# A hybrid attention trunk: the FoX heads' reciprocal row sums go onto the outputs, by a PE transpose and a trip through DRAM, and no longer onto the probabilities

## The chip, the cores and the metric

One core of a Trainium2 chip runs the whole kernel. TensorE (PE) multiplies matrices and turns tiles, VectorE (DVE) and ScalarE (ACT) do elementwise work, and GpSimd (POOL) and SyncE (SP) mostly start transfers. Each engine has a queue of its own and works through it in order; semaphores make one wait for another. The metric is the device time of one execution in microseconds (us), lower is better.

## The reference

A trunk of two layers for one sequence of 512 tokens with 1024 channels, in fp32. Each layer adds half a SwiGLU feed-forward (width 2816), a mixer of two groups of heads, and a second half feed-forward to the residual x. The mixer has 4 differential heads and 8 FoX heads (forgetting attention) of 64 channels. What matters here is a FoX head:

```python
s_f = jnp.einsum('bhqd,bhkd->bhqk', qf, k_f).astype(jnp.float32) * scale_f
s_f = s_f + cf[..., :, None] - cum_f[..., None, :]
s_f = jnp.where(causal, s_f, -jnp.inf)
p_f = jax.nn.softmax(s_f, axis=-1)
o_f = jnp.einsum('bhqk,bhkd->bhqd', p_f.astype(v_f.dtype), v_f)
```

The softmax divides each query's row of exponentials by its sum. The division can stand on the probabilities, one number a query, before the product with v, or on the output after it.

## The kernel before

All fp32 products are made of three matmuls of rounded halves: an operand is split in a high half (a cast on ACT) and a low half (a subtraction on DVE), and hi·hi, hi·lo and lo·hi are summed in a PSUM bank (`mm3`, L386 to L391). Weights stream from DRAM through ring tiles and are split on arrival (L83 on ACT, L84 on DVE). The feed-forwards use a Strassen-like block scheme and take most of the time; PE is all but full there.

In the mixer (`mixer`) the attention of the twelve heads runs in steps, four query blocks of 128 a head, and between the steps PE is given other products, the "filler": the projections of heads still to come (reading XA, the normalised input's halves), FoX's v, and as far as they are ready the output projection's products (`out_early`). A table TARGET says how many filler matmuls should have been issued at each head. The heads come in order, 4 differential ones, then FoX heads 0 to 7. For each step s the loop calls:

- `trans_step(u, kb)` L869: PE turns the probability blocks of key block kb (128x128 each, L874) into one bank; ACT copies it as the high half (L883) and DVE subtracts for the low half (L884). The bank of kb=1 holds three blocks, 384 of its 512 columns.
- `softmax_step(u, qb)` L832: the scores of one query block (L824, L825 and the mask L827), then in the FoX branch DVE adds the forget gates and takes the row minimum (L860, an instruction and the read of its accumulator), ACT takes the exponential with the row sum as accumulator (L862), DVE takes the reciprocal of 128 sums (L863, 128x1) and ACT multiplies the block by it (L864).
- `pv_step(u, kb)`: the output products of key block kb (L913 and L914, v against the high and the low half). After the last, ACT moves a half (L943) and DVE adds it to the other (L944) in the tile `fo["u"]`, 64 partitions a head. The odd head of a pair then has `split_o` cut the pair's tile in halves y (L895 on ACT, L896 on DVE) for the output projection.

Last, `out_rest` multiplies the last pair of heads (6 and 7) and adds the mixer's result to x (L993).

The program order is not the engines' order: a scheduler in the tile layer orders each engine's queue by its own estimates, so a change of a few lines moves other instructions as well. The temporary tiles rotate: five banks for scores, turned blocks and outputs (`ps_b`), three for filler (`ps_a`), six of `t_tile`. SP's queue spreads each head's gates (L857) and loads weights. GpSimd's queue accumulates weight pairs of the feed-forwards (L134) and has nothing to do in FoX's part of the mixer.

Of the kernel before, what the change touches and what calls it, by code (L numbers as in the profile page):

```python
# [8 lines left out]
F32 = mybir.dt.float32  # L9
F32R = mybir.dt.float32r  # L10
BF16 = mybir.dt.bfloat16
AF = mybir.ActivationFunctionType
ALU = mybir.AluOpType
AX = mybir.AxisListType

P = 128
S = 512
# [5 lines left out]
FOX_H = 8  # L23
DIFF_H = 4
NB = S // P
# [22 lines left out]
def rf(t):  # L48
    return t.bitcast(F32)
# [3 lines left out]
def trunk(ctx, tc, xT, x, gains, gain_row, w_gu, w_dn, w_in, w_ff, w_out, fbias, lams, subln, consts, rope, out):  # L53
    nc = tc.nc
    act, dve, pool, pe, sp = nc.scalar, nc.vector, nc.gpsimd, nc.tensor, nc.sync
# [3 lines left out]
    sm = ctx.enter_context(tc.tile_pool(name="sm", bufs=4))  # L59
    ps = ctx.enter_context(tc.tile_pool(name="ps", bufs=1, space=bass.MemoryType.PSUM))  # L60
    dram = ctx.enter_context(tc.tile_pool(name="dram", bufs=2, space=bass.MemoryType.DRAM))
    turn = {}

    def nxt(key, n):
        i = turn.get(key, 0)
        turn[key] = i + 1
        return i % n
# [4 lines left out]
    def home(tag, shape, dt, name):  # L72
        return sb.tile(shape, dt, tag=tag, name=name, bufs=1)

    def t_tile(shape, dt, name, i=None):
        return home(f"t{nxt('t', 6) if i is None else i}", shape, dt, name)
# [139 lines left out]
    for n in range(2 * DEPTH):  # L216
        l = n // 2
        if n % 2 == 1:
            for i in range(24 + len(OUT_K)):
                k = OUT_K[i - 24] if i >= 24 else None  # L220
                tag = MIX[i % 3] if i < 24 else None if k >= 4 else MIX[(i - 28) % 3]
# [44 lines left out]
    ident = const.tile([P, P], F32, name="ident")  # L266
# [316 lines left out]
    def mixer(l, n_next, mid):  # L583
# [11 lines left out]
        pg = [home(f"G{3 + i}", [P, 2048], F32, f"pg{i}") for i in range(2)]  # L595
        PR = {3: 0, 2: 512, 1: 896, 0: 1152}

        def pr_tile(u, qb):
            w = (qb + 1) * P
            return pg[u % 2][:, PR[qb]:PR[qb] + w]  # L600

        def pm_tile():
            return pg[nxt("pm", 2)][:, 1280:1792]
# [212 lines left out]
        units = [("d", h) for h in range(DIFF_H)] + [("f", h) for h in range(FOX_H)]  # L816
        probs = [[] for _ in units]

        def scores(q1, kk, m, qb, masked):
            n = (qb + 1) * P  # L820
            w = max(n, 256)
            p = psum("b")
            lq = q1[m][:, qb * P:n]
            pe.matmul(p[:, 0:w], lq, kk[m][:, 0, 0:w], start=True, stop=False)  # L824
            pe.matmul(p[:, 0:w], lq, kk[m][:, 1, 0:w], start=False, stop=not masked)  # L825
            if masked:
                pe.matmul(p[:, qb * P:n], identb, maskb, start=False, stop=True)  # L827
            return p

        cbs = {}  # L830

        def softmax_step(u, qb):  # L832
            kind, h = units[u]
            n = (qb + 1) * P
            st = sm.tile([P, 6], F32, tag="st", name="st", bufs=6)
            if kind == "d":
                q1, kk = qk[("d", h)]
                pm = []
                for m in range(2):
                    p = scores(q1, kk, m, qb, False)  # L840
                    e = pr_tile(u, qb) if m == 0 else pm_tile()
                    dve.tensor_tensor_reduce(out=e[:, 0:n], in0=p[:, 0:n], in1=maskw[:, S - n:S], op0=ALU.add,
                                             op1=ALU.min, scale=1.0, scalar=3.0e38, accum_out=st[:, m:m + 1])
                    act.activation(out=e[:, 0:n], in_=e[:, 0:n], func=AF.Exp, scale=-1.0, bias=st[:, m:m + 1],
                                   accum_out=st[:, 2 + m:3 + m])
                    pm.append(e)
                dve.reciprocal(out=st[:, 4:6], in_=st[:, 2:4])
                dve.tensor_tensor(out=st[:, 5:6], in0=st[:, 5:6], in1=nlam, op=ALU.mult)
                act.mul(out=pm[1][:, 0:n], in_=pm[1][:, 0:n], mul=st[:, 5:6])
                dve.scalar_tensor_tensor(out=pm[0], in0=pm[0], scalar=st[:, 4:5], in1=pm[1][:, 0:n],  # L850
                                         op0=ALU.mult, op1=ALU.add)
                probs[u].append(pm[0])
            else:
                q1, kk = qk[("f", h // 2)]
                if qb == 0:
                    cbs[h] = rope_t[h % 2]
                    sp.dma_start(out=cbs[h], in_=cum_d[h:h + 1, :].partition_broadcast(P))  # L857
                p = scores(q1, kk, h % 2, qb, True)
                e = pr_tile(u, qb)
                dve.tensor_tensor_reduce(out=e, in0=p[:, 0:n], in1=cbs[h][:, 0:n], op0=ALU.add, op1=ALU.min,  # L860
                                         scale=1.0, scalar=3.0e38, accum_out=st[:, 0:1])
                act.activation(out=e, in_=e, func=AF.Exp, scale=-1.0, bias=st[:, 0:1], accum_out=st[:, 2:3])  # L862
                dve.reciprocal(out=st[:, 4:5], in_=st[:, 2:3])  # L863
                act.mul(out=e, in_=e, mul=st[:, 4:5])  # L864
                probs[u].append(e)

        pts = {}
# [1 line left out]
        def trans_step(u, kb):  # L869

            w = S - kb * P
            p = psum("b")
            for qb in range(kb, NB):
                pe.transpose(p[:, (qb - kb) * P:(qb - kb + 1) * P], probs[u][qb][:, kb * P:(kb + 1) * P], ident)  # L874
            if kb == NB - 1:
                th, tl = pt3
                dst = slice(P, 2 * P)
                full = (th, tl, slice(256, S))
            else:
                th, tl = pair()  # L880
                dst = slice(0, w)
                full = (th[:, 0:w], tl[:, 0:w], slice(kb * P, S))
            act.copy(out=th[:, dst], in_=p[:, 0:w])  # L883
            dve.tensor_tensor(out=tl[:, dst], in0=p[:, 0:w], in1=rf(th[:, dst]), op=ALU.subtract)  # L884
            pts[(u, kb)] = full
# [5 lines left out]
        fo = {}  # L891

        def split_o(i, u):
            oh, ol = y_pair(i)
            act.copy(out=oh, in_=u)  # L895
            dve.tensor_tensor(out=ol, in0=u, in1=rf(oh), op=ALU.subtract)  # L896
            ovt[i] = (oh, ol)

        def pv_step(u, kb):
            kind, h = units[u]  # L900
            if kb == 0:
                po_[u] = psum("b")
            po = po_[u]
            th, tl, cols = pts.pop((u, kb))
            hs = slice(h * P, (h + 1) * P)
            if kind == "d":
                vh, vl = vd[kb]
                pe.matmul(po[:, cols], vh[:, hs], th, start=kb == 0, stop=False)
                pe.matmul(po[:, cols], vl[:, hs], th, start=False, stop=False)
                pe.matmul(po[:, cols], vh[:, hs], tl, start=False, stop=kb == NB - 1)  # L910
            else:
                v = vf[kb][:, hs]
                pe.matmul(po[:, cols], v, th, start=kb == 0, stop=False)  # L913
                pe.matmul(po[:, cols], v, tl, start=False, stop=kb == NB - 1)  # L914
            if kb < NB - 1:
                return
            po_.pop(u)
            if kind == "d":
                o = os_[h // 2][:, h % 2]
                act.copy(out=o, in_=po)  # L920
                sq = t_tile([P, S], F32, "osq")
                act.activation(out=sq, in_=po, func=AF.Square)
                sh_, sl_ = pair()
                act.copy(out=sh_, in_=sq)
                dve.tensor_tensor(out=sl_, in0=sq, in1=rf(sh_), op=ALU.subtract)
                ov[h] = o

                def stats():
                    pq = psum("b")
                    pe.matmul(pq[0:32], ones[:, 0:32], sh_, start=True, stop=False)  # L930
                    pe.matmul(pq[0:32], ones[:, 0:32], sl_, start=False, stop=True)
                    act.activation(out=vv[32 * h:32 * h + 32], in_=pq[0:32], func=AF.Identity, scale=1.0 / P,
                                   bias=eps_t[0:32])
                    if h == DIFF_H - 1:
                        diff_norm()
                later.append(stats)
            else:
                if h % 2 == 0:
                    fo["u"] = pm_tile()
                own = slice(64 * (h % 2), 64 * (h % 2) + 64)  # L940
                oth = slice(64 - 64 * (h % 2), P - 64 * (h % 2))
                t = t_tile([P, S], F32, "fot")
                act.copy(out=t[own], in_=po[oth])  # L943
                dve.tensor_tensor(out=fo["u"][own], in0=po[own], in1=t[own], op=ALU.add)  # L944
                if h % 2 == 1:
                    split_o(h // 2, fo["u"])

        later = []
# [135 lines left out]
        for s in range(4 * len(units) + 5 + LAG):  # L1084
            u, i = divmod(s, 4)
# [6 lines left out]
            v, kb = divmod(s - 4 - LAG, 4)  # L1092
# [8 lines left out]
            v, kb = divmod(s - 5 - LAG, 4)  # L1101
# [327 lines left out]
```

## Time and profile before

| | |
|---|---|
| median of 3 runs | 1869.1 us (1868.81 to 1869.91) |
| profiled execution | 1871.02 us, its span 1869.2 us |
| granted TensorE clock, mean | 0.996 |
| scales on ACT (L864), both layers | 64, 35.9 us |
| reciprocals of 128x1 on DVE (L863) | 64, 10.2 us |
| transposes of probability blocks on PE (L874) | 240, 46.1 us |
| first output product of FoX head 0, layer 1 | 499 us from the span's start |
| last addition of head 7 (L944), layer 1 | 572.38 us |

A row of a group gives the line, the engine, the operation, out<-in tiles, the shapes and the count, then the busy time in us, the mean of one in ns, and the engine's idle time just before them with what ended it. A row of the timeline gives the start, the duration, the engine and the instruction; in brackets stands the idle time before it and what released it. A row of windows gives the length of a stretch and the busy time of each engine with its number of instructions, then the clock, the share of the DMA engines and GB/s. PE's matmuls are pipelined and their ends are modelled, so a busy PE may still wait; the distance between two starts is the better price.

### The profile page before, as it was taken

The page shows a single profiled execution, that of the slowest core. Times are in us where ns is not written, and L with a number is a line of the kernel's source. Part 1 is how long each engine was busy: PE and PEld are TensorE (multiplying, and loading weights), DVE is VectorE, ACT ScalarE, POOL GpSimd, SP SyncE. Part 2 cuts the span into 40 slices and gives each one's busy share as a digit, 9 for nine tenths or more (in the row PEclk, how much of TensorE's full clock was granted, in tenths as well). Part 3 has the DMA queues.
Part 4 walks back from the last instruction along what each step waited for, and adds up shares of the span by engine and source line. Part 5 has one row for each costly group of instructions (what it writes and reads, how often), then busy time and mean ns, then how long its engine had stood idle before and what let it go on. Part 6 is the DMA issues. An engine that isn't in the chain of part 4 may idle for free.

```text
span 1869.2 us, 24488 instructions
## 1 busy us (share of the span) xinstructions
PE 1833.9 (98%) x8702; PEld 1496.0 (80%) x8702; DVE 1611.6 (86%) x2528; ACT 1133.3 (61%) x1795; POOL 128.2 (7%) x154
## 2 busy tenths in 40 slices
PE   9999999999999999999999999999999999999997
PEld 5888888778868889888778988877777788888886
DVE  7898898778686999898998989997876869898998
ACT  7556555557795755565575556545576957455564
POOL 2010000000000100100001000000000000000101
PEclk9999999999999999999999999999999999999999
DMA  9787655243336775777567667533433466856742
GB/s 308 207 224 191 189 143 145 91 130 108 105 96 184 203 203 149 196 210 195 135 181 206 171 166 205 158 111 108 117 104 103 127 175 188 216 143 186 221 114 89
DMA packets 95529, 303.79 MB, mean 163 GB/s; under 512 B 12568, under 2 KB 15128, under 8 KB 95408
## 3 DMA queue, kind: packets, MB, share of 16 engines
q1 hardware_dynamic: 74816, 232.15, 37.1%
q0 software_dynamic: 19296, 68.17, 20.4%
q10 hardware_dynamic: 1296, 1.93, 0.4%
q8 instruction: 68, 1.11, 0.2%
q14 instruction: 53, 0.43, 0.1%
HBM read 287.45 MB, written 2.16 MB: 155 GB/s over the span
## 4 chain that ended last, share of the span: by engine, by line
PE 83%; DVE 9%; ACT 5%; DMA 2%; issue 1%; SPq 0%; DVEq 0%; ACTq 0%
PE ps_c L389 12%; PE ps_c L390 12%; PE ps_c L391 12%; PE ps L389 9%; PE ps L390 9%; PE ps L391 9%; PE ps_a L389 3%; PE ps_a L390 3%; PE ps_a L391 3%; DVE wg L84 2%; PE ps_t L485 2%; DVE x L514 1%; PE ps_g L1248 1%; PE ps_a L665 1%; PE ps_a L666 1%; PE ps_a L667 1%
## 5 line engine op out<-in xcount | busy, mean ns | idle before, releaser
L83 ACT CAST wg<-raw 128x1024 fp32r<-128x1024 f32 (+1 forms) x525 | 537.9, 1031 | 486.5 <-PE ps_c L391 188.9
L84 DVE TENSOR_TENSOR wg<-raw,wg 128x1024 fp32r<-128x1024 f32 (+1 forms) x525 | 619.7, 1190 | 105.5 <-ACT wg L83 104.0
L389 PE MATMUL ps_c<-wg,xf 128*128 128x512 f32 (+1 forms) x736 | 277.8, 378 | 2.2 <-ACT wg L83 1.3
L390 PE MATMUL ps_c<-wg,xf 128*128 128x512 f32 (+1 forms) x736 | 277.1, 377 | 1.0 <-DVE wg L84 1.0
L391 PE MATMUL ps_c<-wg,xf 128*128 128x512 f32 (+1 forms) x736 | 276.2, 376 | 0.0
L389 PE MATMUL ps<-wg,xf 128*128 128x512 f32 (+1 forms) x552 | 210.2, 381 | 0.0
L390 PE MATMUL ps<-wg,xf 128*128 128x512 f32 (+1 forms) x552 | 207.2, 376 | 0.0
L391 PE MATMUL ps<-wg,xf 128*128 128x512 f32 (+1 forms) x552 | 206.7, 376 | 0.0
L389 PEld LDWEIGHTS ps_c<-wg,xf 128*128 128x128 f32 x736 | 138.6, 188 | 29.2 <-ACT wg L83 1.7
L390 PEld LDWEIGHTS ps_c<-wg,xf 128*128 128x128 f32 x736 | 138.9, 189 | 26.5 <-DVE wg L84 1.5
L391 PEld LDWEIGHTS ps_c<-wg,xf 128*128 128x128 f32 x736 | 138.9, 189 | 25.1
L134 POOL DMA_DIRECT2D raw<-w_gu x86 | 74.6, 867 | 1137.8 <-DMA raw<-w_gu 640.3
L389 PE MATMUL ps_c<-wg,hf 128*128 128x512 f32 x352 | 138.5, 394 | 5.9 <-DVE x L514 5.8
L390 PE MATMUL ps_c<-wg,hf 128*128 128x512 f32 x352 | 137.4, 390 | 0.0
L391 PE MATMUL ps_c<-wg,hf 128*128 128x512 f32 x352 | 137.2, 390 | 0.0
L514 DVE SCALAR_TENSOR_TENSOR x<-ps_c,x 128x512 f32<-128x512 f32 x192 | 123.9, 680 | 1.3 <-PE ps_c L391 1.2
L391 PEld LDWEIGHTS ps<-wg,xf 128*128 128x128 f32 x552 | 103.8, 188 | 18.9
L389 PEld LDWEIGHTS ps<-wg,xf 128*128 128x128 f32 x552 | 103.9, 188 | 18.0 <-ACT xf L83 0.4
L390 PEld LDWEIGHTS ps<-wg,xf 128*128 128x128 f32 x552 | 104.0, 188 | 17.6
L389 PE MATMUL ps_a<-XA,wg 128*128 128x512 f32 x256 | 106.1, 415 | 1.9 <-ACT XA L343 1.8
L390 PE MATMUL ps<-wg,hf 128*128 128x512 f32 x264 | 103.1, 390 | 0.0
L389 PE MATMUL ps<-wg,hf 128*128 128x512 f32 x264 | 103.1, 390 | 0.0
(286 smaller groups left out, 3545.4 us busy)
## 6 DMA issues: line engine op xcount, KB each, us to landing
raw<-w_gu SPq DMA_DIRECT2D x218, 512.0 KB, 4.4
raw<-w_dn SPq DMA_DIRECT2D x100, 512.0 KB, 4.3
raw<-w_gu POOLq DMA_DIRECT2D x86, 512.0 KB, 6.8
raw<-w_in SPq DMA_DIRECT2D x48, 512.0 KB, 3.3
raw<-w_dn POOLq DMA_DIRECT2D x40, 512.0 KB, 5.6
kdup<-qk_t SPq DMA_DIRECT2D x64, 128.0 KB, 2.4
raw<-w_out SPq DMA_DIRECT2D x16, 512.0 KB, 3.2
raw<-w_dn SPq DMA_DIRECT2D x20, 256.0 KB, 6.0
```

The source lines that it names most:

```text
L83: act.copy(out=hi, in_=src)
L84: dve.tensor_tensor(out=lo, in0=src, in1=rf(hi), op=ALU.subtract)
L134: pool.dma_start(out=t, in_=where(two, h)[1], accum_op=ALU.add)
L389: pe.matmul(p, lh, rh, start=start, stop=False, skip_group_check=again)
L390: pe.matmul(p, lh, rl, start=False, stop=False, skip_group_check=again)
L391: pe.matmul(p, ll, rh, start=False, stop=stop, skip_group_check=again)
L485: pe.transpose(pj[j][:, e * 256 + p * P:e * 256 + (p + 1) * P], hs[j][p][:, o:o + P], ident)
L514: dve.scalar_tensor_tensor(out=xc, in0=src, scalar=scale, in1=xc, op0=ALU.mult, op1=ALU.add)
L665: pe.matmul(pv[t], xh[:, ts], wh[:, sl], start=k == 0, stop=False)
L666: pe.matmul(pv[t], xh[:, ts], wl[:, sl], start=False, stop=False)
L667: pe.matmul(pv[t], xl[:, ts], wh[:, sl], start=False, stop=k == KT - 1)
L1248: pe.matmul(pg[2 * half + j], gained(kp, e, half)[:, j * P:(j + 1) * P], w0[kp][:, e * S:(e + 1) * S], start=kp + e == 0, stop=kp == KP - ...
```

## The change

The exponentials stay unscaled. Their row sums are accumulated in one tile of four columns a head (`fsum`, a column for each query block). When the head's kb=1 bank is filled, `row_sums` has PE turn the 128x4 sums into the bank's free corner (4 partitions, the last 128 columns), DVE takes the reciprocal from there into a temporary (4x128), and GpSimd's queue writes it to DRAM as a row of 512 and reads it back twice, each time 256 columns spread over the head's 64 partitions, into the columns 1792 to 2047 of two large tiles (`rb_h`). After the odd head's output the pair's tile is multiplied by them (two multiplications of 128x256), and then split as before.

```diff
+        sums_ = {}
+        rs_d = dram.tile([FOX_H, S], F32, name="rs_d")
+        rb_h = [t[:, 1792:2048] for t in pg]
+
+        def row_sums(h, p):
+
+            pe.transpose(p, sums_.pop(h), ident)
+            rr = t_tile([P, S], F32, "rr")
+            dve.reciprocal(out=rr[0:NB, 0:P], in_=p)
+            pool.dma_start(out=rs_d[h].rearrange("(q p) -> q p", p=P), in_=rr[0:NB, 0:P])
+            own = slice(64 * (h % 2), 64 * (h % 2) + 64)
+            for c in range(2):
+                pool.dma_start(out=rb_h[c][own], in_=rs_d[h:h + 1, c * 256:c * 256 + 256].partition_broadcast(64))
...
-                act.activation(out=e, in_=e, func=AF.Exp, scale=-1.0, bias=st[:, 0:1], accum_out=st[:, 2:3])
-                dve.reciprocal(out=st[:, 4:5], in_=st[:, 2:3])
-                act.mul(out=e, in_=e, mul=st[:, 4:5])
+                if qb == 0:
+                    sums_[h] = sm.tile([P, NB], F32, tag="fsum", name="fsum", bufs=2)
+                act.activation(out=e, in_=e, func=AF.Exp, scale=-1.0, bias=st[:, 0:1],
+                               accum_out=sums_[h][:, qb:qb + 1])
...
+            if kb == 1 and units[u][0] == "f":
+                row_sums(units[u][1], p[0:NB, S - P:S])
             act.copy(out=th[:, dst], in_=p[:, 0:w])
...
                 if h % 2 == 1:
+                    for c in range(2):
+                        uc = fo["u"][:, c * 256:c * 256 + 256]
+                        dve.tensor_tensor(out=uc, in0=uc, in1=rb_h[c], op=ALU.mult)
                     split_o(h // 2, fo["u"])
```

Over both layers 64 scales on ACT and 64 reciprocals of 128x1 on DVE go; 16 transposes on PE, 16 reciprocals of 4x128 and 32 multiplications on DVE, and 48 transfers on GpSimd's queue come. Lines move: in the changed kernel the reciprocal of the sums is L840, the transfers L841 and L844, DVE's work on the scores L874, the exponential L878, the turned blocks' halves L900 and L901, the outputs' halves L960 and L961, the multiplications L965, y's low half L913 and the addition to x L1013.

How the order moves. The first place is ACT's queue in layer 1 around the end of head 2. Before:

```order
L862 ACTIVATE pg_2798,st<-pg_2798,st 128x128 [waits DVE_49]
L883 CAST pair<-ps_b 128x512 [waits PE_49]
L864 ACTIVATE pg_2798<-pg_2798,st 128x128 [waits DVE_49]
L862 ACTIVATE pg_2798,st<-pg_2798,st 128x256
L943 COPY fot<-ps_b 64x512 [waits DMAHW1_49]
L883 CAST pair<-ps_b 128x384 [waits PE_49]
L862 ACTIVATE pg_2798,st<-pg_2798,st 128x384
L864 ACTIVATE pg_2798<-pg_2798,st 128x256 [waits DVE_49]
L883 CAST pair<-ps_b 128x256 [waits PE_49]
L883 CAST pt_0_95<-ps_b 128x128 [waits PE_49]
```

And the same place of the changed kernel:

```order
L878 ACTIVATE pg_2798,fsum<-pg_2798,st 128x128 [waits DVE_49]
L900 CAST pair<-ps_b 128x512 [waits PE_49]
L878 ACTIVATE pg_2798,fsum<-pg_2798,st 128x256 [waits DVE_49]
L960 COPY fot<-ps_b 64x512 [waits DMAHW2_49,PE_49]
L900 CAST pair<-ps_b 128x384 [waits DVE_49,Activation_49]
L900 CAST pair<-ps_b 128x256 [waits PE_49]
L900 CAST pt_0_95<-ps_b 128x128 [waits PE_49,Activation_49]
L878 ACTIVATE pg_2798,fsum<-pg_2798,st 128x384 [waits DVE_49]
```

The scales are gone, and the copy of 384 columns, the kb=1 bank, waits for DVE where it waited for PE. The second place is DVE's queue in layer 1 around the end of head 3, in the changed kernel; `pg` is the tile of a pair's output as well as of probabilities, and DMASW are GpSimd's transfers. Head 3's own reciprocal stands 15 instructions ahead of the first row, and the L840 here is head 4's:

```order
L840 RECIPROCAL rr<-ps_b 4x128 [waits DMASW3_49,PE_49]
L901 TENSOR_TENSOR pair<-ps_b,pair 128x512 [waits DVE_49,Activation_49]
L961 TENSOR_TENSOR pg_2799<-ps_b,fot 64x512 [waits Activation_49]
L901 TENSOR_TENSOR pair<-ps_b,pair 128x384 [waits Activation_49]
L965 TENSOR_TENSOR pg_2799<-pg_2799,pg_2798 128x256 [waits DMASW7_49,DMASW2_49,DVE_49]
L965 TENSOR_TENSOR pg_2799<-pg_2799 128x256 [waits DMASW3_49,DMASW0_49]
L874 ISA pg_2799,st<-ps_b,rope 128x384 [waits PE_49]
L874 ISA st 128x1
L84 TENSOR_TENSOR XA_2701<-raw,XA_2701 128x1024
L913 TENSOR_TENSOR y_2800<-pg_2799,y_2800 128x512 [waits Activation_49]
```

Behind the two multiplications stand head 5's scores and a low half of XA that before stood ahead of head 2's last addition; of these there are now four between L961 of heads 2 and 6, where the trace of before has two in the time from head 2 to head 6. PE's order has 44 filler matmuls between the first output products of heads 2 and 6, before 34. Between the end of head 1's kb=1 bank and its pair's end PE has 34 of them. The third place is DVE's queue at the end of layer 1's heads 6 and 7. Before:

```order
L944 TENSOR_TENSOR pg_2799<-ps_b,fot 64x512 [waits Activation_49]
L884 TENSOR_TENSOR pair<-ps_b,pair 128x384 [waits Activation_49]
L884 TENSOR_TENSOR pair<-ps_b,pair 128x256 [waits DVE_49,Activation_49]
L884 TENSOR_TENSOR pt_1_96<-ps_b,pt_0_95 128x128 [waits Activation_49]
L944 TENSOR_TENSOR pg_2799<-ps_b,fot 64x512 [waits Activation_49]
L896 TENSOR_TENSOR y_2800<-pg_2799,y_2800 128x512 [waits Activation_49]
L84 TENSOR_TENSOR wg<-raw,wg 128x1024 [waits DMAHW6_49,Activation_49]
```

And after:

```order
L840 RECIPROCAL rr<-ps_b 4x128 [waits PE_49]
L961 TENSOR_TENSOR pg_2799<-ps_b,fot 64x512 [waits Activation_49]
L901 TENSOR_TENSOR pair<-ps_b,pair 128x384 [waits Activation_49]
L901 TENSOR_TENSOR pair<-ps_b,pair 128x256 [waits DVE_49,Activation_49]
L901 TENSOR_TENSOR pt_1_96<-ps_b,pt_0_95 128x128 [waits DVE_49,Activation_49]
L961 TENSOR_TENSOR pg_2799<-ps_b,fot 64x512 [waits Activation_49]
L965 TENSOR_TENSOR pg_2799<-pg_2799,pg_2798 128x256 [waits DMASW6_49,DMASW3_49,DVE_49]
L965 TENSOR_TENSOR pg_2799<-pg_2799 128x256 [waits DMASW7_49,DMASW4_49]
L84 TENSOR_TENSOR wg<-raw,wg 128x1024 [waits DMAHW4_49,Activation_49]
L913 TENSOR_TENSOR y_2800<-pg_2799,y_2800 128x512 [waits Activation_49]
```

Head 7's reciprocal and its multiplications have five instructions between them, and a weight's low half and y's stand behind. On PE 18 matmuls stand between head 7's last output product and the first that reads the last y.

## The prediction

> **What bounds the kernel now.** I read the page first for the shares, then the windows (busy time of each engine) around the FoX heads' attention, then the waits in the stretch where PE idles, and last the groups of that stretch by shape.
>
> ```profile
> PE 1833.9 (98%) x8702; PEld 1496.0 (80%) x8702; DVE 1611.6 (86%) x2528; ACT 1133.3 (61%) x1795; POOL 128.2 (7%) x154
> ```
>
> Over the whole span PE is the bound and ACT has 39% to spare, so taking 64 scales off ACT looks worthless. But these are averages. The next rows cut layer 1 at the first output product (L913, 128x512) of heads 2 and 6; the last windows row is the same stretch of layer 2.
>
> ```profile
> 525.29 0.49 PE L913 MATMUL ps_b<-pair,vf 128*128 128x512 f32 x1
> 556.09 0.50 PE L913 MATMUL ps_b<-pair,vf 128*128 128x512 f32 x1 [0.87 <-ACT pair L883]
> ```
>
> ```profile
> core 0: us, PE busy (x) PEld busy (x) DVE busy (x) ACT busy (x) POOL busy (x), PEclk, DMA share, GB/s
> 500.00:525.29 25.29, 25.29 (x135) 20.25 (x133) 20.38 (x52) 19.96 (x43) 0.00 (x0) 1.00 0.39 126
> 525.29:556.09 30.80, 27.43 (x155) 20.50 (x154) 26.92 (x82) 30.36 (x79) 0.00 (x0) 1.00 0.32 95
> 556.09:575.00 18.91, 18.50 (x87) 14.15 (x88) 13.57 (x22) 13.53 (x25) 0.86 (x1) 1.00 0.69 224
> 1452.13:1483.31 31.18, 28.16 (x155) 21.46 (x155) 26.72 (x81) 30.45 (x79) 0.00 (x0) 0.95 0.31 94
> ```
>
> In the first and third stretch PE is the bound: it idles 0 and 0.41 us. In the second ACT works 30.36 of 30.80 us (99%), DVE 26.92 (87%), PE shows 3.37 us idle. Layer 2 repeats it: ACT 30.45 of 31.18. So there are two stretches, 62 us in all, where ACT sets the pace; only there can ACT's relief move the end. The waits of the layer-1 stretch say the same: PE and its weight loads stand for ACT.
>
> ```profile
> PEld ps_b L913 <- ACT pair L883: 1.9, 4, 1.1
> PEld ps_b L874 <- ACT pg L864: 1.6, 3, 1.3
> PE ps_b L874 <- ACT pg L864: 0.9, 1, 0.9
> PE ps_b L913 <- ACT pair L883: 0.8, 1, 0.8
> ```
>
> **What is removed.** In that stretch:
>
> ```profile
> L864 ACT ACTIVATE pg<-pg,st 128x512 f32<-128x512 f32 x4 | 2.9, 728 | 0.0
> L864 ACT ACTIVATE pg<-pg,st 128x256 f32<-128x256 f32 x5 | 2.5, 507 | 0.0
> L864 ACT ACTIVATE pg<-pg,st 128x384 f32<-128x384 f32 x4 | 2.5, 617 | 0.0
> L864 ACT ACTIVATE pg<-pg,st 128x128 f32<-128x128 f32 x4 | 1.6, 398 | 0.0
> L863 DVE RECIPROCAL st<-st 128x1 f32<-128x1 f32 x17 | 2.7, 160 | 1.0 <-ACT pg L862 0.8
> L84 DVE TENSOR_TENSOR XA<-raw,XA 128x1024 fp32r<-128x1024 f32 x2 | 2.4, 1214 | 0.1
> ```
>
> ACT loses 2.9 + 2.5 + 2.5 + 1.6 = 9.5 us and falls to 20.9 of 30.8; it stops being the bound. DVE loses 17 reciprocals, 2.7 us by their durations; a window counts overlapped instructions once, so it loses between half of that, 1.4, and all. Elsewhere both savings lie beside a busy PE and count nothing.
>
> **What is late next: DVE.** It was at 26.92 and gets four reciprocals of 4x128 and, for two pairs of heads, four multiplications 128x256 (L965). Prices:
>
> ```profile
> L491 DVE TENSOR_TENSOR ws<-hb,ps_t 128x256 f32<-128x256 f32 x44 | 18.3, 415 | 13.3 <-ACT ws L490 13.3
> L316 DVE RECIPROCAL nst<-nst 128x4 f32<-128x4 f32 x6 | 1.0, 172 | 2.0 <-ACT nst L315 2.0
> L728 DVE RECIPROCAL zt<-zt 128x32 f32<-128x32 f32 x2 | 0.7, 344 | 0.0
> L874 PE MATMUL ps_b<-ident,pg 128*128 128x128 f32 x240 | 46.1, 276 | 2.0 <-ACT pg L864 1.9
> 508.40 0.28 PE L824 MATMUL ps_b<-qk 128*128 128x256 f32 x1
> 508.52 0.28 PE L825 MATMUL ps_b<-qk 128*128 128x256 f32 x1
> ```
>
> Multiplications: 4 × 0.415 = 1.7 us. The reciprocal is the hidden price. One column (160 ns) and four (172) cost almost the same, but 32 cost 344: 172 ns for 28 columns more, 6.1 ns each. Turned, the same 512 sums are 4 partitions of 128 columns, and by that slope one takes 344 + 96 × 6.1 = 930 ns, more than the four of 160 that it replaces. No row shows it: the ends are 0.34 and 0.93 us, and I take the slope, since the rows show no flattening. Four are 3.7 us. DVE comes to 26.9 − (1.4 to 2.7) + 3.7 + 1.7 = 29.6 to 30.9; I take 30.2, as full as ACT was. So the stretch loses 30.8 − 30.2, **−0.6 us**; in layer 2, with 26.72 + 3.3 = 30.0 of 31.18, **−1.2 us**. ACT's 9.5 us are all but paid back by DVE.
>
> **Work that the order moves.** Between the first output products of heads 2 and 6 PE now has 44 filler matmuls, before 34, and DVE all four low halves of XA, before two. Ten matmuls of 0.235 us (571.57 to 572.04 for two, below) leave stretches where PE has no idle time for one where it has: −2.3 us; two halves of 1.21 come into DVE's: +2.4. I take **0** for both.
>
> **What is added on PE.** Eight transposes a layer of a 4-column operand. Start to start a 256-column matmul costs 0.12 us (508.40 to 508.52), a whole transpose with its modelled end 0.276. Four fall in the stretch, where PE has idle time; the other four cost 0.5 to 1.1 us, and PE's own rate is the start-to-start one: **+0.5**.
>
> **The new wait at the block kb=1.** ACT's copy of that bank (L900) now waits for DVE's reciprocal. Behind it in ACT's queue stand the copies of kb=2 and kb=3 and the next exponentials, and PE's output products wait for the copies. It costs nothing where ACT has slack, and at most a reciprocal each, 8 × 0.93 = 7.4 us a layer. ACT has 10 us of slack in the stretch, and DVE, which then is the bound, isn't held up; I take **+0.3**, near the lower end.
>
> **The way through DRAM.** Per head the row goes from GpSimd's queue to DRAM (2 KB), then twice back, 64 KB each. SP's queue is not touched; GpSimd's is empty here (0 busy from 500 to 556). The odd head's multiplications stand in DVE's queue and wait for the landings; behind them stand the next heads' score reads (L874), the low halves (L901) and at the end y's low half. The round trip R, from the reciprocal's end:
>
> ```profile
> raw<-w_dn POOLq DMA_DIRECT2D x8, 256.0 KB, 4.2
> nd<-v_d SPq DMA_DIRECT2D x2, 8.0 KB, 1.8
> L134 POOL DMA_DIRECT2D raw<-w_gu x86: 856/862/1037, 20.9 to 1769.5; - x86
> 508.36 0.48 SPq L962 DMA_DIRECT2D ms_d<-nd  x1
> 510.73 0.33 SPq L966 DMA_DIRECT2D rbd<-ms_d  x1
> 513.95 0.75 DVE L968 SCALAR_TENSOR_TENSOR ou<-o,sub_s,rbd 128x512 f32<-128x512 f32 x1
> ```
>
> Low end: two small landings of 1.8 and one GpSimd issue of 0.86, 4.5 us. High end: two of GpSimd's 256 KB landings and an issue, 2 × 4.2 + 0.86 = 9.3 us. The nearest row is the diff heads' own write-and-spread on SP, issued at 508.36 and first read at 513.95: I take **R = 5.6**. The Trainium skill, page "DMA: Bandwidth & Descriptors", section "Anatomy of one DMA — SWDGE (gpsimd) path", gives a transfer from GpSimd's queue a fixed 2.0 us plus its bytes over 436 GB/s, an estimate of 4.2 us for the two in chain, which would take the 1.2 us a layer of the tail, below, off the sum; this trace's 256 KB landing of 4.2 us, where that fit gives 2.6, does not agree.
>
> What covers R? For head 3 the order has 18 DVE instructions between its reciprocal and its pair's first multiplication; at the stretch's mean of 26.92/82 = 0.328 us, with one of them a reciprocal of 0.93, 6.5 us. Head 5 has 16, two of them XA's of 1.21 us, which is no less. Head 1 has 34 filler matmuls, where PE is the bound. There R = 5.6 is hidden. Head 7 has five DVE instructions and the tail:
>
> ```profile
> 567.81 0.38 PE L874 MATMUL ps_b<-ident,pg 128*128 128x128 f32 x2
> 571.57 0.40 PE L389 MATMUL ps_b<-wg,y 128*128 128x512 f32 x1
> 572.04 0.39 PE L391 MATMUL ps_b<-wg,y 128*128 128x512 f32 x1
> 573.11 0.62 ACT L895 CAST y<-pg 128x512 fp32r<-128x512 f32 x1 [0.76 <-DVE pg L944]
> 573.76 0.69 DVE L896 TENSOR_TENSOR y<-pg,y 128x512 fp32r<-128x512 f32 x1 [0.69 <-ACT y L895]
> ```
>
> The kb=1 transposes start at 567.81; the reciprocal may begin at about 568.3 and end at 569.2. After the last output product the order leaves PE 18 matmuls until the first that reads this y: 571.57 + 18 × 0.235 = 575.8. Ahead of that lie two multiplications (0.83), the high half (0.62) and for the next matmul but one the low half (0.69), so the multiplications must start by about 573.6, 4.4 us after the reciprocal. R = 5.6 then costs **+1.2** a layer.
>
> **Sum.** Layer 1: −0.6 + 0 + 0.5 + 0.3 + 1.2 = +1.4. Layer 2: −1.2 + 2.0 = +0.8. Together +2.2 us. The profiled execution took 1871.0 us (span 1869.2, 1.8 outside), 1.9 above the median of 1869.1; the same step goes onto either, so the median becomes **1871.3 us**. About 0.2%, 3.7 us, is what a measurement of this kernel can tell from no change: I forecast none that shows. This case's own range, from R hidden at the tail (−2.4) to the reciprocals' wait at 1 us a layer (+1.4), is 1868.9 to 1872.7.
>
> **Rivals.**
>
> *DVE's overflow goes next door, and PE takes over (faster).* DVE is 81% busy in the stretch ahead and 72% in the one behind, 4.9 and 5.3 us of slack, and the chain from exponential to transpose loses two steps (its reciprocals idled 1.0 us for L862). Then the stretch shrinks to PE's own work. Weight loads are 20.50 us there; ahead, where PE never idled, 25.29 us held 20.25 of loads, so 20.50 needs 25.6. That frees 5.2 us; 20.50, loads alone, would free 10.3. With 7 less the costs of 2.0, −5 a layer: **1859**. A reciprocal of 0.34 alone (DVE at 27.8) takes 2.4 off the forecast in the stretch and 0.6 at the tail, a layer: 1865. For it: ACT's 9.5 us are truly gone. Against it: DVE's queue is in order, and its 30 us stand in the stretch.
>
> *The round trip is late (slower).* Place: L965 in DVE's queue at heads 3 and 5, and the tail. Covers are 6.5, 6.5 and 4.4 us; the tail decides first. From R = 6.4 the tail costs 0.8 a layer more and the loss shows; from 6.5 on it is 3R − 17.4 a layer, and DVE, full by then, gives nothing back. If each of three GpSimd issues waits out one DVE instruction of 0.69 us, R is 5.6 + 2.1 = 7.7: 5.7 a layer, 4.5 more than in the sum: **1880**. At R = 9.3 it is 10.5, 1890. For it: nothing but DVE's own work hides L965. Against it: GpSimd's issues took 856 to 1037 ns with DVE 86% busy. The Trainium skill, "SBUF — State Buffer", section "SBUF: two separate sides", warns that a DMA of GpSimd's queue starves of descriptors while DVE holds the shared port in a two-port mode; that would be this rival, and by the issue times the trace does not show it.
>
> *DVE gets XA's halves and PE gives nothing back.* If the ten matmuls moved only fill waits that were hidden by others, the +2.4 stays: +2.4 a layer on the forecast, **1876**. Against it: the halves stand ahead of the matmuls that read them, both moved together.
>
> *The change does nothing where it should.* If the stretch isn't ACT's after all, only costs remain, 2.0 a layer: 1873. Against it is 99% busy.
>
> **How the numbers follow.** Forecast 0.40, PE takes over or cheap reciprocals 0.28, the late trip 0.20, XA's halves or costs alone 0.12. Faster by over 0.2% (below 1865.4): 0.27 of the second and 0.03 of the first, 0.30. Slower (above 1872.8): 0.20 + 0.10 + 0.03 of the forecast, 0.33. Same: 0.37. The range goes from PE's case, 1859, to the late trip at 7.7, 1880; beyond each end lies a part of that rival, 0.1 each.
>
> **What would show it.** Right: from head 2 to head 6 ACT falls to near 21 us, DVE is over 95% busy, the time of it hardly moves; L840 takes 0.9 us; L965 waits for a DMA at head 7 alone. Wrong: L965 idle over a microsecond at heads 3 or 5 (late trip); L840 at 0.4 us, or PE without idle time there (PE takes over); L900 waiting long for L840; neither engine full and the stretch as long as before.

## The result and the profile after

| | median us | runs | ratio to before, 95% interval |
|---|---|---|---|
| before | 1869.51 | 4 (1868.81 to 1870.22) | |
| changed | 1887.68 | 4 (1885.32 to 1889.38) | 1.0100, 1.0088 to 1.0112 |

The change makes the kernel 18.2 us slower, 1.0%. The profiled spans are 1884.9 and 1869.2 us, 15.7 apart, with mean clocks of 0.992 and 0.996. The page's first line shows what was moved and nothing of the loss:

```profile
PE 1838.9 (98%) x8718; PEld 1501.4 (80%) x8718; DVE 1621.7 (86%) x2496; ACT 1107.1 (59%) x1731; POOL 154.7 (8%) x202
```

The windows of the changed kernel show it. The first two rows are the heads' stretches of the prediction, from head 2's first output product to head 6's, in layer 1 and 2; the third is the tail, from the end of head 7's reciprocal to the last multiplication.

```profile
523.07:558.35 35.28, 31.47 (x171) 24.17 (x170) 31.56 (x74) 26.57 (x66) 6.26 (x12) 0.95 0.37 109
1457.80:1491.42 33.62, 29.66 (x170) 22.96 (x170) 31.23 (x74) 26.47 (x66) 6.28 (x12) 1.00 0.37 110
...
569.30:581.50 12.20, 7.64 (x37) 6.00 (x35) 2.88 (x7) 2.44 (x5) 3.40 (x5) 0.92 0.88 279
```

The same 12.2 us of the kernel before:

```profile
569.30:581.50 12.20, 12.20 (x57) 9.89 (x56) 6.40 (x11) 4.81 (x8) 3.45 (x4) 1.00 0.96 304
```

PE, full before, now idles 4.56 us there, with nearly all other engines idle beside it. Read the last two columns too: the 16 DMA engines are 88% busy. They move the next feed-forward's weights, 279 GB/s, where they were 37% busy from head 2 to head 6. This traffic is not new, the kernel before has 96% there; new is a trip that runs beside it. Layer 1's waits in that time name the chain:

```profile
ACT wg L83 <- DVE pg L965: 7.2, 1, 7.2
DVE pg L965 <- DMA pg<-rs_d: 6.9, 2, 6.0
PEld ps_a L389 <- ACT y L912: 6.1, 1, 6.1
...
PE ps_a L389 <- ACT y L912: 5.7, 1, 5.7
```

DVE's multiplications stand and wait for the spread reciprocals, PE for the y that they give, and ACT's copy of the last weight of w_out for the tile in which they landed (the weight ring takes `pg` over, the landing place included). The timeline of this tail, row by row:

```profile
568.39 0.94 DVE L840 RECIPROCAL rr<-ps_b 4x128 f32<-4x128 f32 x1 [0.65 <-PE ps_b L838]
...
569.62 0.51 POOL L841 DMA_DIRECT2D rs_d<-rr  x1 [6.00 <-DVE rr L840]
...
573.50 0.69 DVE L961 TENSOR_TENSOR pg<-ps_b,fot 64x512 f32<-64x512 f32 x1 [2.09 <-ACT fot L960]
573.65 1.06 POOL L844 DMA_DIRECT2D pg<-rs_d  x2 [3.52 <-DMA rs_d<-rr]
...
580.23 0.42 DVE L965 TENSOR_TENSOR pg<-pg,pg 128x256 f32<-128x256 f32 x1 [6.03 <-DMA pg<-rs_d]
581.52 0.42 DVE L965 TENSOR_TENSOR pg<-pg 128x256 f32<-128x256 f32 x1 [0.88 <-DMA pg<-rs_d]
```

The reciprocal ends at 569.33; the first multiplication starts 10.9 us later, the second 12.2. The write took 4.0 us from its issue to the next transfer, the spread another 6.6. What PE did in this time:

```profile
576.55 0.39 PE L391 MATMUL ps_b<-wg,y 128*128 128x512 f32 x1
582.65 0.79 PE L389 MATMUL ps_a<-wg,y 128*128 128x512 f32 x1 [5.72 <-ACT y L912]
```

At 0.23 us from start to start PE would have needed the last y at about 576.8. Ahead of that lie the two multiplications and y's high half (0.62 us), so the first multiplication had to start by about 575.3, 6.0 us after the reciprocal: this is PE's cover, estimated from the rows above. The loss does not end with the wait:

```profile
582.60:586.60 4.00, 3.94 (x10) 3.03 (x11) 2.44 (x4) 1.05 (x2) 0.11 (x1) 0.52 1.08 219
```

Right behind it the granted clock is 0.52, in layer 2 0.51, and the matmuls start 0.43 us apart in place of 0.23.

Layer 2's trip took 11 us as well: two more waits of the same kind are in the sum over the whole kernel, four in all. The rows of the multiplications, of the two transfers' landings (of L841, then of L844) and of the reciprocal:

```profile
  DMA pg<-rs_d: 13.4, 4
```

```profile
DMA to landing us min/median/max: 1.5/1.6/4.6
```

```profile
DMA to landing us min/median/max: 2.5/3.0/7.2
```

```profile
L840 DVE RECIPROCAL rr<-ps_b x16: 934/939/946, 494.0 to 1501.7; 4x128 f32<-4x128 f32 x16
```

The median landing is that of a quiet stretch, the longest that of the tail. No other head's multiplication waited.

### The profile page after: what moved, and what is told of

It is laid out like the page before. It is cut to its first block, busy times and chain, and to the rows that moved or that the text cites. A ratio compares the mean times of both kernels' runs of the same rounds, so it can differ in the third digit from the quotient of the medians.

```text
span 1884.9 us, 24576 instructions
## 1 busy us (share of the span) xinstructions
PE 1838.9 (98%) x8718; PEld 1501.4 (80%) x8718; DVE 1621.7 (86%) x2496; ACT 1107.1 (59%) x1731; POOL 154.7 (8%) x202
## 4 chain that ended last, share of the span: by engine, by line
PE 84%; DVE 9%; DMA 2%; ACT 2%; issue 2%; POOL 0%; DVEq 0%; ACTq 0%; POOLq 0%
PE ps_c L389 12%; PE ps_c L391 12%; PE ps_c L390 12%; PE ps L391 8%; PE ps L390 8%; PE ps L389 8%; PE ps_a L389 4%; PE ps_a L390 4%; PE ps_a L391 3%; DVE wg L84 2%; PE ps_t L485 2%; DVE x L514 2%; PE ps_g L1268 1%; PE ps_a L665 1%; PE ps_a L667 1%
## 5 line engine op out<-in xcount | busy, mean ns | idle before, releaser
L134 POOL DMA_DIRECT2D raw<-w_gu x86 | 74.9, 871 | 628.7 <-DVE wg L84 161.9
L389 PE MATMUL ps_a<-XA,wg 128*128 128x512 f32 x256 | 106.2, 416 | 1.5 <-ACT XA L343 1.2
L390 PE MATMUL ps<-wg,hf 128*128 128x512 f32 x264 | 103.3, 391 | 0.0
L390 PE MATMUL ps_a<-XA,wg 128*128 128x512 f32 x256 | 102.0, 399 | 1.3 <-DVE XA L344 1.2
```

Source lines behind the costliest of these rows:

```text
L134: pool.dma_start(out=t, in_=where(two, h)[1], accum_op=ALU.add)
L389: pe.matmul(p, lh, rh, start=start, stop=False, skip_group_check=again)
L390: pe.matmul(p, lh, rl, start=False, stop=False, skip_group_check=again)
```

## The experiments

The theory after this reading: head 7's late trip is nearly all of the loss, and it is late because the weights fill the DMA engines. Rivals: GpSimd's own way of issuing is slow; or DVE's added work is the loss, and the tail would wait for something else without it.

**no_wait_h7**, the tail's wait alone:

```diff
+        rb_x = sb.tile([P, 256], F32, tag="rbx", name="rbx", bufs=1)
...
-                pool.dma_start(out=rb_h[c][own], in_=rs_d[...])
+                pool.dma_start(out=(rb_h[c] if h < 6 else rb_x)[own], in_=rs_d[...])
```

> The change whole, but the transfers of heads 6 and 7 land in a tile of their own that nobody reads, and the last pair of outputs is multiplied by the numbers of heads 4 and 5, long landed (the last pair's scale is thus not its own). Every queue's order is that of the changed kernel; only the wait of the last two multiplications goes. Theory (the loss is the wait for head 7's trip through DRAM, about 6 us a layer of idle PE, and the rest of some 1.6 us a layer is DVE's): 1887.7 - 12 = 1876 us, 1874 to 1878. Rival (DVE's added work, 0.94 us reciprocals and the multiplications, is the main loss, and the tail would have waited for something else): above 1883 us.

Measured: 1870.28 us, ratio 1.0007 (0.9997 to 1.0016). PE's, DVE's, ACT's and SP's orders are those of the changed kernel. The tail, 12 us of it:

```profile
569.00:581.00 12.00, 12.00 (x56) 9.58 (x55) 8.07 (x14) 4.95 (x9) 2.24 (x4) 1.00 0.94 311
```

PE is full again, at a clock of 1.00. 17.4 of the 18.2 us hang on this trip, and the rest of the change comes out even. That refutes DVE's work as the cause of this loss. It is more than the 12 us expected. PE's order is the same in both traces, so the start of each matmul can be set beside its counterpart's: the waits of the two layers put the changed kernel 11.6 us behind, and the slow matmuls right behind them another 4.4, together 16.0 of the 16.8 us between the spans. That the wait itself brings the clock down was not tested on its own; here and in sp_h7, where PE doesn't wait, the clock of this stretch is 1.00. What is removed is both the wait of L965 and that of the weight's copy, since the transfers no longer land in `pg`. GpSimd's order does differ: the two landings share one tile, so the second waits for the first, and weight pairs go out between them.

**sp_h7**, the queue:

```diff
-            pool.dma_start(out=rs_d[h] ...
+            q = sp if h == 7 else pool
+            q.dma_start(out=rs_d[h] ...
...
-                pool.dma_start(out=rb_h[c][own] ...
+                q.dma_start(out=rb_h[c][own] ...
```

> Head 7's three transfers on SP's queue, all others on GpSimd's. Theory (the transfers are late because the DMA engines are 88% busy with the next feed-forward's weights): they stand on SP's queue behind those very weights, L965's idle time at head 7 stays above 4 us and the time above 1883 us. Rival (GpSimd's own way of issuing is slow): the trip falls to the 5.6 us that the differential heads' trip takes on SP, L965 idles under 1 us, and the time is 1876 to 1878 us.

Measured: 1871.15 us, ratio 1.0012 (1.0002 to 1.0021). My theory of the weights alone falls here, and the rival's 5.6 us are not reached either. The timeline of its tail:

```profile
568.51 0.95 DVE L840 RECIPROCAL rr<-ps_b 4x128 f32<-4x128 f32 x1 [0.68 <-PE ps_b L838]
...
569.48 0.27 SPq L842 DMA_DIRECT2D rs_d<-rr  x1
569.86 2.53 SPq L101 DMA_DIRECT2D raw<-w_gu  x2
572.48 1.11 SPq L845 DMA_DIRECT2D pg<-rs_d  x2
...
576.30 0.42 DVE L966 TENSOR_TENSOR pg<-pg,pg 128x256 f32<-128x256 f32 x1 [2.01 <-DMA pg<-rs_d]
```

Among the same weights, on their own queue, the trip takes 6.8 us (569.46 to 576.30) in place of 10.9: write 3.0, spread 3.8. DVE still idles 2.0 us, and the time barely shows it: 0.9 us more than with no wait at all. The shorter trip is not the whole reason. PE's order is another here: nine matmuls that do not read the last y stand ahead of the first that does, where the changed kernel has them behind it. At 0.23 us each they add 2.1 us to the cover of 6.0. In the changed kernel's order PE would still have waited some 1.4 us in layer 1, by an estimate from these rows (y's high half is ready 8.9 us after the reciprocal, and PE runs out 7.5 us after it).

**weights_held**, the traffic:

```diff
         for o in range(0, cols, w):
+            if gate:
+                sp.dma_start(out=t[64:65, 0:64], in_=gate[0][64:65, 0:64])
             sp.dma_start(out=t[:, o:o + w], in_=src[:, o:o + w])
...
-                if i < early and running:
+                if i < early and running and not (late and early > 3):
```

(`gate` holds the landed tile during `out_rest`, `late` is set from `out_early` to there.)

> The next feed-forward's weights are held back: all but three of the loads that run beside head 7's trip now wait on SP's queue until the trip has landed (a small transfer out of the landed tile into each weight tile stands ahead of its load). Theory (the trip is late because of these loads): from the end of head 7's reciprocal to the first multiplication about 6 us instead of 10.9, L965 idle under 2 us. Rival (GpSimd's way is slow by itself): 10 us or more, as before. The whole time tells little, since the feed-forward then starts with late weights: 1875 to 1895 us.

Measured, a single run: 1885.62 us. The tail's rows:

```profile
566.73 0.95 DVE L844 RECIPROCAL rr<-ps_b 4x128 f32<-4x128 f32 x1 [0.66 <-PE ps_b L842]
...
567.97 0.51 POOL L845 DMA_DIRECT2D rs_d<-rr  x1 [6.00 <-DVE rr L844]
...
571.72 1.06 POOL L848 DMA_DIRECT2D pg<-rs_d  x2 [3.24 <-DMA rs_d<-rr]
...
575.60 0.43 DVE L969 TENSOR_TENSOR pg<-pg,pg 128x256 f32<-128x256 f32 x1 [3.07 <-DMA pg<-rs_d]
```

The trip takes 7.9 us on GpSimd's queue. The write, beside the three loads that I could not hold (issued from 567.89), stays at 3.8 us; the spread, with the others held, falls from 6.6 to 3.9. L965 (L969 here) idles 3.1 us, over the 2 that I expected, and the trip lies between the theory's 6 and the rival's 10. The DMA engines were not free: their share is 0.75 during the spread, in the changed kernel 0.92. So GpSimd's queue and the weights' traffic together make 11 us, and SP's queue or less traffic leaves 7 to 8. How much of this is the queue's own stays open. The write is shorter on SP's queue in every tail of this record (2.5 to 3.0 us, GpSimd's 3.9 to 5.0 with no load held). The spread is not always: SP's took 3.8 and 4.8 us in sp_h7, but 5.3 and 6.5 in recip_first_sp below, against 6.6 and 6.0 in the changed kernel. In the changed kernel's layer 1 two of GpSimd's own weight pairs (L134) also leave right behind the spread, and their part was not separated.

**removal_only**: the scales and the reciprocals of 128x1 go and nothing comes (`row_sums`, its call and L965 are left out), so the outputs are not divided by their sums.

> The scales and the 128x1 reciprocals are taken out and nothing is put in their place: the outputs of the FoX heads are not divided by their sums. This is the most that ACT's relief can bring. If ACT was the bound from head 2 to head 6 and PE's own work is next, the stretch loses 4 to 7 us a layer: 1856 to 1862 us. If the relief is hidden anyway: within 2 us of 1869.5.

Measured: 1854.67 us, ratio 0.9922 (0.9907 to 0.9937). Layer 1 from head 2's first product to head 6's:

```profile
520.25:552.23 31.98, 31.30 (x182) 24.79 (x181) 29.57 (x71) 28.75 (x70) 0.00 (x0) 1.00 0.39 119
```

The stretch is not shorter: the order has moved more filler into it. But PE gets through 182 matmuls in 31.98 us, where before's 30.80 us held 155, and idles 0.7 us in place of 3.4. The relief is real and worth 15 us, ACT's scales and DVE's 64 reciprocals together.

**mult_only**: removal_only with the multiplications by a tile of ones.

```diff
+                    for c in range(2):
+                        uc = fo["u"][:, c * 256:c * 256 + 256]
+                        dve.tensor_tensor(out=uc, in0=uc, in1=rb_1, op=ALU.mult)
                     split_o(h // 2, fo["u"])
```

> The bare removal plus the two multiplications 128x256 a pair, by a tile of ones written once at the start: no sums, no turning, no transfers, no wait. Theory (DVE's work counts by its length): 1854.7 + 4 to 7 = 1859 to 1862 us. Rival (the multiplications are the main cost): above 1864 us.

Measured: 1856.03 us, ratio 0.9927 (0.9912 to 0.9942). There are 16 multiplications, two for each of the four pairs of a layer; the 32 in the description of the change and in the expectation of sums_no_mult is a miscount. They cost 1.4 us, about a fifth of their durations' 6.7 (16 of 0.418), and less than either theory said; the intervals of the two runs overlap.

**sums_no_mult**: the change without L965 (its loop is deleted).

> The change without the multiplications L965: sums turned, reciprocals of 4x128 taken and sent through DRAM, and nobody reads them (outputs undivided). Of the 15.0 us that the bare removal brings, this shows what the turning, the reciprocals and ACT's wait for them take. Theory (DVE is the bound in ACT's place, its 16 reciprocals of 0.94 us are 15 us and the multiplications' 32 x 0.34 another 11): the reciprocals take the larger part, 1854.7 + 8 to 11 = 1863 to 1866 us. Rival (DVE's queue is held up by the multiplications' place in it, not by the reciprocals): under 1859 us.

Measured: 1882.80 us, ratio 1.0071 (1.0055 to 1.0088). Far from both: nobody reads the spread numbers, and the loss is there still. Its waits from 560 us on say why:

```profile
ACT wg L83 <- DMA pg<-rs_d: 6.3, 1, 6.3
PEld ps_a L389 <- ACT wg L83: 5.7, 1, 5.7
```

The weight tile that takes `pg` over has to wait for the landing, reader or not. The late trip holds PE by two chains in parallel, y and the last weight of w_out; taking away one alone brings little. It was no measure of the reciprocals.

**recip_first_sp**, the reciprocals' form, on top of sp_h7:

```diff
+                if qb == NB - 1:
+                    dve.reciprocal(out=sums_[h], in_=sums_[h])
...
-            dve.reciprocal(out=rr[0:NB, 0:P], in_=p)
+            act.copy(out=rr[0:NB, 0:P], in_=p)
```

> As sp_h7 (head 7's transfers on SP's queue), and the reciprocal is taken of the 128x4 sums before they are turned (0.17 us in place of 0.94); ACT moves the turned 4x128 out of the bank. Theory: DVE has 16 x 0.77 = 12 us less, some half of it in stretches where it is the bound, and the tail's trip starts 0.6 us earlier: 1871.2 - 5 to 8 = 1863 to 1866 us. Rival (DVE isn't the bound, the wait of the kb=1 copy is): the copy then waits for nothing, and the gain is the same or smaller; if the loss lay in the multiplications alone, no gain, 1870 us or more.

Measured: 1861.87 us, ratio 0.9961 (0.9948 to 0.9974): 9.3 us under sp_h7. The same 512 reciprocals, one instruction again, the sums on 128 partitions:

```profile
L882 DVE RECIPROCAL fsum<-fsum x16: 158/172/179, 478.7 to 1482.4; 128x4 f32<-128x4 f32 x16
```

SP's trip, from the end of ACT's copy, takes 8.2 and 9.0 us in the two layers here, and PE is busy all through it: the nine matmuls stand ahead in this order too.

**recip_first**, the same edit on the change itself:

> The change whole, all transfers on GpSimd's queue, with one edit: the reciprocal is taken of the 128x4 sums before the turn (0.17 us instead of 0.94) and ACT moves the turned row out of the bank. Theory (two separate losses: about 9 us by DVE's reciprocals as recip_first_sp against sp_h7 showed, and some 16 us by the late trip, which stays): 1887.7 - 9 - up to 1.2 for the earlier start = 1877 to 1879 us. Rival (the two overlap, so that the tail takes back what the reciprocals give): 1884 us or more.

Measured: 1875.99 us, ratio 1.0037 (1.0023 to 1.0051), 11.7 us under the change. The two losses are separate in the main: taking the reciprocals first gains 11.7 us with the late trip and 9.3 on top of sp_h7. The trip is as late as ever:

```profile
574.47 0.43 DVE L967 TENSOR_TENSOR pg<-pg,pg 128x256 f32<-128x256 f32 x1 [7.14 <-DMA pg<-rs_d]
```

**pe_spread**, no DRAM at all:

```diff
+        SPREAD = {1: (0, 1), 2: (2, 4), 3: (1, 2)}
...
+        def spread(h, kb, p, w):
+            a, b = SPREAD[kb]
+            for q in range(a, b):
+                pe.transpose(p[:, w + (q - a) * P:w + (q - a + 1) * P], sums_[h][:, q:q + 1].broadcast_to([P, P]),
+                             ident)
+            own = slice(64 * (h % 2), 64 * (h % 2) + 64)
+            o = a % 2 * P
+            act.copy(out=rb_h[a // 2][own, o:o + (b - a) * P], in_=p[own, w:w + (b - a) * P])
...
+                if qb == NB - 1:
+                    dve.reciprocal(out=sums_[h], in_=sums_[h])
...
+            if kb and units[u][0] == "f":
+                spread(units[u][1], kb, p, w)
```

> No DRAM: reciprocals of the 128x4 sums, then PE turns each column, read 128 times over, into the free corners of the kb=1, 2 and 3 banks, so that each of 128 output rows holds the reciprocals of 128 queries; ACT copies them out (three copies a head, 0.9 us), and the multiplications stay on DVE. No transfer, so no late one. Theory: PE +48 transposes a layer less 8, DVE 12 us less, no wait at the tail: 1860 to 1865 us, faster than before. Rival (the tail needs the spread numbers earlier than ACT can bring them, or ACT is full again with 7 us a layer more): 1868 us or more.

Measured: 1866.76 us, ratio 0.9986 (0.9976 to 0.9995). A little faster than before, but 4.9 us behind recip_first_sp and outside what I expected. It puts 32 transposes a layer on PE (the text on record says 48, a slip) in place of 8, and three copies a head on ACT; by the 0.12 us of the prediction the 24 more a layer are 5.8 us in both layers. That would explain the distance, but no run separates it from the copies.

**last_pair_old**: heads 6 and 7 keep their scales on ACT.

```diff
+                if h >= 6:
+                    act.activation(out=e, in_=e, func=AF.Exp, scale=-1.0, bias=st[:, 0:1], accum_out=st[:, 2:3])
+                    dve.reciprocal(out=st[:, 4:5], in_=st[:, 2:3])
+                    act.mul(out=e, in_=e, mul=st[:, 4:5])
...
-            if kb == 1 and units[u][0] == "f":
+            if kb == 1 and units[u][0] == "f" and units[u][1] < 6:
...
-                    for c in range(2):
+                    for c in range(2 if h < 6 else 0):
```

> The change for heads 0 to 5 alone; heads 6 and 7 have their probabilities scaled as before, so nothing waits for a trip at the tail. Theory (the late trip of head 7 is some 17 us of the loss, and ACT has room for the last two heads): 1868 to 1871 us, no change from before. Rival (trips of earlier heads cost too): 1874 us or more.

Measured: 1870.59 us, ratio 1.0009 (1.0000 to 1.0018), as expected: no multiplication waits for a landing any more, in either layer, and the rest of the change comes out even.

**last_pair_old_recip_first**, both edits:

> As last_pair_old, and the reciprocals are taken of the 128x4 sums before the turn. Theory: the gain of the two edits adds, 1870 - 9 less a little, since only 12 of 16 heads are turned: 1860 to 1864 us, faster than before and than the change. Rival (scaling two heads on ACT is late at the end): 1866 us or more.

Measured: 1859.80 us, ratio 0.9954 (0.9940 to 0.9967), the fastest version with all of the reference's work in it, 27.9 us under the change and 8.9 us under the median of its own runs of before, 1868.71. Its layer 1, in two windows:

```profile
525.00:556.00 31.00, 30.30 (x174) 23.96 (x173) 29.32 (x78) 28.51 (x71) 6.25 (x12) 1.00 0.45 128
...
569.00:581.00 12.00, 12.00 (x55) 9.92 (x54) 4.40 (x6) 3.77 (x6) 3.54 (x4) 1.00 0.99 278
```

PE idles 0.7 us in the first, and the tail is full.

## Why the prediction was wrong

It forecast 1871.3 us, no change that shows, within 1859 to 1880; 1887.7 was measured. The direction was the late rival's. It had R at 7.7 and a part of its loss at heads 3 and 5, where nothing waited, and came to 1880.

**The step that failed: R = 5.6, at the tail +1.2 a layer.** I took one round trip for all heads, from the differential heads' trip at 508 to 514 us, where the windows row shows a DMA share of 0.39 (500 to 525). The trip that decides runs at 569, and the prediction's own row for 556 to 575 says 0.69. I quoted that column and didn't read it. R at the tail was 10.9 (first multiplication) to 12.2 us (second), above even my high end of 9.3, which was built of two landings of 256 KB on GpSimd's queue. The tail cost 17.4 us in both layers together (no_wait_h7), in place of 2.4. Some 12 of it are the waits; about 4 are PE at half its clock behind them, a term that the sum does not have. The step also missed a second waiter: the landing place is part of `pg`, and the next weight tile waits for it (sums_no_mult). And GpSimd's queue, which I took as empty from a window that ends at 556 us, issues weight pairs of the next feed-forward from 574 us on. The sign that I named for being right, L965 waiting for a DMA at head 7 alone, came true; it says where the wait is and not how long it is.

**The cover at the tail, 4.4 us.** About 6.0 by the rows of the tail: too low, but on the safe side.

**Heads 1, 3 and 5 hidden.** Right: no L965 waited there. In quiet stretches the landings, 1.6 and 3.0 us, and an issue of 0.53 between the two spreads come to some 5 us.

**The reciprocal, 0.93 us by the slope of 4 to 32 columns.** Right, 0.939. With the wait of the kb=1 copy for it, it ate most of the gain: taking it before the turn brought 11.7, 9.3 and 10.8 us in three pairs of kernels (the last is last_pair_old against last_pair_old_recip_first).

**ACT's relief paid back by DVE, the rest of the sum near nothing.** Right in the sum, by luck: without the tail's 2.4 I had −0.2, no_wait_h7 measured +0.6 against its own runs of before. The gain and its price were each sized too small, and the two errors cancel. The bare relief is 15.0 us, near the 14 that the rival "PE takes over" assumed for both layers, where the sum, after DVE's share, had 1.8; the reciprocals are ten or so of what is lost again. The multiplications are 1.4 us, about a fifth of their durations. The few us that are left of the sum no run assigns. DVE reached 89% of the longer stretch (31.56 of 35.28), not 95%, and ACT 26.6 us, not 21, with filler and its halves of XA moved in. The stretch from head 2 to head 6 did not keep its length, 30.8, but took 35.3; part of that is PE's 16 further instructions (171 against 155).

**The new wait of the kb=1 copy.** In the changed kernel ACT's copy waits for the reciprocal twice, 1.8 us in all, at head 7 of each layer; I had 0.6. What this costs was not tested apart from the reciprocal: recip_first removes both.

**GpSimd held up by DVE.** The form in which I put the slow rival, each issue delayed by a DVE instruction, is not what happened. At the tail the issues took 0.51 and 1.06 us for two, as elsewhere; the delay lies between issue and landing, and DVE stood idle for 6.0 of the spread's 6.6 us.

## What to carry to other kernels

Price a transfer from the stretch in which it will run: read the DMA share of that window first, and where a small transfer runs beside weight streams, look at who waits at the end of it, since a trip hidden in seven heads out of eight cost everything in the eighth. Before a row of sums is turned to save instructions, do the slow elementwise operation while it still lies across the partitions: 128x4 took 0.17 us, 4x128 took 0.94. Ask who gets the landing place next, besides who reads it. And look at PE's clock behind a long wait: here it made 12 us of waiting into 16.

## What the runs showed of the hardware

A DVE reciprocal costs by columns: 172 ns at 4, 344 at 32, 939 at 128, about 6.2 ns each. The number of partitions did not show: 64x32 took 340 ns and 128x32 344, and 4x128 lies on the same slope.

Beside a weight stream with the DMA engines 88% busy a small write from GpSimd's queue took 4.0 us (in layer 2 4.9) and a spread of 64 KB 6.6 (6.0); GpSimd's same transfers land in 1.6 and 3.0 us where the share is near 0.37. From SP's queue, among the weights, the write took 2.5 to 3.0 us and the spread 3.8 to 6.5.

Behind waits of PE of nearly 6 us its granted clock was 0.52 and 0.51 for the next 4 to 6 us, and matmuls of 512 columns started 0.43 us apart in place of 0.23. Without the wait (no_wait_h7) the clock there was 1.00.
